# Scattering the expert gates: products of four tokens side by side in PSUM, part of the marks on ScalarE, small marks for 48 tokens

## The chip, the cores and the metric

The kernel runs on one core of one Trainium2 chip. The metric is the device time of one execution in microseconds. TensorE does the matmuls and writes PSUM; VectorE (DVE), ScalarE (ACT) and GpSimd (POOL) work on 128 partitions at a time; SyncE (SP) issues most DMAs. Each engine runs its own instructions in order, and the engines wait for one another through semaphores.

## The reference

Two transformer blocks over 512 tokens of width 1024. The changed code lies in the feed-forward layer of the first, a product-key mixture of 16384 experts:

```
s = einsum('thpc,hpnc->thpn', q, keys)            # two scores of 128 keys for each of 8 heads
v1, i1 = top_k(s[:, :, 0], 16);  v2, i2 = top_k(s[:, :, 1], 16)
sc, pos = top_k(v1[..., :, None] + v2[..., None, :], 16)     # over 256 pairs
idx = (i1 * 128 + i2) at pos;  gate = softmax(sc)
act = gelu(einsum('td,thkd->thk', x, u_tab[idx]))
out = einsum('thk,thkd->td', gate * act, v_tab[idx])
```

So each token chooses 8 x 16 = 128 experts, each with two coordinates (i1, i2) of 0 to 127 and a gate.

## The kernel before

For three of the four blocks of 128 tokens (ND = 384) the kernel does not gather expert rows. It runs all experts densely: for each of 128 values of the second coordinate, `up` makes the 128 x 384 products with `pe_u` and their Gelu, `dense` multiplies them with the gates and with `pe_v`. For that it needs the gates as a full matrix of 128 x 128 experts for each token, zero where an expert is not chosen. `scatter` builds it.

At its start `slots` holds, with the 128 chosen experts on the partitions and the 384 tokens along the row: 0 the gate, 1 and 2 the upper three bits (0 to 7) and the lower four bits (0 to 15) of the first coordinate, 3 the second coordinate. `iota` is a row of 0 to 127. For a token, `e[0]` is the matrix (chosen expert x first coordinate) with the gate at the mark, `e[1]` the matrix (chosen expert x second coordinate) with a one at the mark. One TensorE matmul of the two sums over the chosen experts and gives the 128 x 128 gates of this token.

The loop goes over 24 blocks of 16 tokens (`t16`) and in each over 4 quads of four tokens (`q`), 96 quads in all:

- per block, on VectorE: `g` (L518, L522), the upper bits' marks times the gates, 16 x 8 numbers, and `lw` (L520), the lower bits' marks, 16 x 16 in bf16;
- per quad, on VectorE: `e[1]` (L527), a comparison of 4 x 128 elements, and `e[0]` (L529), the product of `g` and `lw` spread over 4 x 8 x 16 elements. The two tiles have three buffers each;
- per quad, on TensorE: four f32 matmuls of 128 x 128 into one PSUM bank `p` (L534). In the trace each is two records. Four banks (role `gp`) take turns;
- per quad, on ScalarE: three copies of 10 values of the second coordinate each to `gm` (L537), which stays in SBUF for the first RES = 30 values, and one copy of the other 98 to `out` (`go`, L538). In SBUF the token is the innermost index, in `p` the second coordinate is, so these copies write single f32 apart from each other;
- per block, SP's queue stores `out` to DRAM (L540). `dense` loads it later in groups (L549 to L552).

The generator yields after each quad, and `interleave` puts the remaining steps of `fill` between the quads. `fill` is `ahead`: the `up` work of the first EARLY = 26 values of the second coordinate, 24 f32r matmuls each, with the load and split of its weights (L62, L64, L67) and a Gelu (L566). The program is then ordered for each engine by a scheduler with its own estimate of the durations, so quads and `up` work need not follow each other as the loop has them. When the last quad is copied, `dense` begins: L608 multiplies the early Gelus with rows of `gm`, each a row of all 384 tokens.

Of the kernel before, what the change touches and what calls it, by code (L numbers as in the profile page):

```python
# [13 lines left out]
F32 = mybir.dt.float32  # L14
# [3 lines left out]
BF16 = mybir.dt.bfloat16  # L18
AF = mybir.ActivationFunctionType
ALU = mybir.AluOpType  # L20
# [327 lines left out]
ND = 384  # L348
NB = ND // 16
RES, GRP = 30, 8  # L350
# [70 lines left out]
class Peer:  # L421
# [84 lines left out]
    def scatter(self, wk, ps, slots, pool, iota):  # L506

        k, nc = self.k, self.k.nc
        V, A, G, T = nc.vector, nc.scalar, nc.gpsimd, nc.tensor
        for t16 in range(NB):
            ts = slice(16 * t16, 16 * t16 + 16)
            g = pool.tile([128, 16, 8], F32, name=k.name("gu"), tag="gu")
            lw = pool.tile([128, 16, 16], BF16, name=k.name("lw"), tag="lw")
            out = pool.tile([128, 128 - RES, 16], F32, name=k.name("go"), tag="go")
            V.tensor_tensor(out=g, in0=slots[:, 1, ts].unsqueeze(2).to_broadcast([128, 16, 8]),  # L518
                            in1=iota[:, 0:8].unsqueeze(1).to_broadcast([128, 16, 8]), op=ALU.is_equal)
            V.tensor_tensor(out=lw, in0=slots[:, 2, ts].unsqueeze(2).to_broadcast([128, 16, 16]),  # L520
                            in1=iota[:, 0:16].unsqueeze(1).to_broadcast([128, 16, 16]), op=ALU.is_equal)
            V.tensor_tensor(out=g, in0=g, in1=slots[:, 0, ts].unsqueeze(2).to_broadcast([128, 16, 8]), op=ALU.mult)  # L522
            for q in range(4):
                o = 16 * t16 + 4 * q
                e = [wk.tile([128, 512], F32, name=k.name("e"), tag=tag, bufs=3).rearrange("p (t n) -> p t n", t=4)
                     for tag in ("alo", "ahi")]
                V.tensor_tensor(out=e[1], in0=slots[:, 3, o:o + 4].unsqueeze(2).to_broadcast([128, 4, 128]),  # L527
                                in1=iota.unsqueeze(1).to_broadcast([128, 4, 128]), op=ALU.is_equal)
                V.tensor_tensor(out=e[0].rearrange("p t (u l) -> p t u l", u=8),  # L529
                                in0=g[:, 4 * q:4 * q + 4].unsqueeze(3).to_broadcast([128, 4, 8, 16]),  # L530
                                in1=lw[:, 4 * q:4 * q + 4].unsqueeze(2).to_broadcast([128, 4, 8, 16]), op=ALU.mult)
                p = ps.tile([128, 4, 128], F32, name=k.name("gp"), tag="gp")
                for i in range(4):
                    T.matmul(p[:, i, :], e[0][:, i, :], e[1][:, i, :], start=True, stop=True)  # L534
                n = RES // 3
                for z in range(3):
                    A.copy(self.gm[z][:, :, o:o + 4].rearrange("p n t -> p t n"), p[:, :, n * z:n * z + n])  # L537
                A.copy(out[:, :, 4 * q:4 * q + 4].rearrange("p n t -> p t n"), p[:, :, RES:])  # L538
                yield
            nc.sync.dma_start(self.gd[t16], out.rearrange("p n t -> p (n t)"))  # L540

# [1652 lines left out]
```

## Time and profile before

| | us |
|---|---|
| median of 3 runs | 3055.88 (3053.62 to 3061.26) |
| the profiled execution's own time | 3059.69 |
| its span, first to last instruction | 3057.9 |
| PE busy | 2931.2 (96%) |
| DVE busy | 2066.5 (68%) |
| ACT busy | 1374.2 (45%) |
| POOL busy | 645.4 (21%) |

An engine's busy time is the sum over all stages. Since the stages have different limits, a stage is read from the windows, which give each engine's busy time in a stretch, and from the chain of waits, which goes back from the last instruction to what released it. In the lists a group has the line of the kernel, the engine, the operation, the tile written and those read, the shapes and the count. Starts of successive instructions on one engine can lie closer together than the recorded duration, since an instruction begins before the last results of the one ahead are written.

### The profile page before, as it was taken

The page shows a single profiled execution, that of the slowest core. Times are in us where ns is not written, and L with a number is a line of the kernel's source. Part 1 is how long each engine was busy: PE and PEld are TensorE (multiplying, and loading weights), DVE is VectorE, ACT ScalarE, POOL GpSimd, SP SyncE. Part 2 cuts the span into 40 slices and gives each one's busy share as a digit, 9 for nine tenths or more (in the row PEclk, how much of TensorE's full clock was granted, in tenths as well). Part 3 has the DMA queues.
Part 4 walks back from the last instruction along what each step waited for, and adds up shares of the span by engine and source line. Part 5 has one row for each costly group of instructions (what it writes and reads, how often), then busy time and mean ns, then how long its engine had stood idle before and what let it go on. Part 6 is the DMA issues. An engine that isn't in the chain of part 4 may idle for free.

```text
span 3057.9 us, 45818 instructions
## 1 busy us (share of the span) xinstructions
PE 2931.2 (96%) x17602; PEld 2489.1 (81%) x17602; DVE 2066.5 (68%) x4031; ACT 1374.2 (45%) x2543; POOL 645.4 (21%) x435
## 2 busy tenths in 40 slices
PE   8888989998899999999999999989999999999999
PEld 6766779997688999999999987668888877888887
DVE  6877768989997888888886446675552653655522
ACT  5444453357533333333333355664442554554422
POOL 0000014400004444444442011002222121012220
PEclk9898999999999999999999999999999999999999
DMA  2000252243349999999996432323223442133222
GB/s 96 26 21 30 80 182 92 90 149 151 151 147 329 342 334 334 340 337 330 331 334 243 130 116 70 110 91 105 97 97 104 161 133 92 53 105 97 97 96 83
DMA packets 177787, 481.86 MB, mean 158 GB/s; under 512 B 18944, under 2 KB 68864, under 8 KB 177312
## 3 DMA queue, kind: packets, MB, share of 16 engines
q1 hardware_dynamic: 140704, 344.70, 33.3%
q0 software_dynamic: 36864, 134.23, 12.1%
q8 instruction: 138, 2.26, 0.3%
q14 instruction: 81, 0.66, 0.1%
HBM read 454.36 MB, written 24.51 MB: 157 GB/s over the span
## 4 chain that ended last, share of the span: by engine, by line
PE 74%; DVE 7%; ACT 1%; issue 1%; DMA 1%; POOL 0%; DVEq 0%; ACTq 0%
PE pacc L119 6%; PE pu L117 6%; PE pu L119 6%; PE pu L118 6%; PE pacc L118 5%; PE pacc L117 5%; PE up L118 5%; PE up L119 5%; PE up L117 5%; PE acc L117 3%; PE acc L118 3%; PE acc L119 3%; PE pj L117 2%; PE pj L118 2%; PE pj L119 2%; PE sp L805 2%
## 5 line engine op out<-in xcount | busy, mean ns | idle before, releaser
L64 ACT CAST whi<-raw 128x1024 fp32r<-128x1024 f32 x505 | 529.6, 1050 | 686.8 <-PE pu L118 184.0
L67 DVE TENSOR_TENSOR wlo<-raw,whi 128x1024 fp32r<-128x1024 f32 x394 | 487.9, 1240 | 473.6 <-ACT whi L64 468.0
L67 POOL TENSOR_TENSOR wlo<-raw,whi 128x1024 fp32r<-128x1024 f32 x111 | 273.2, 2463 | 1057.1 <-ACT whi L64 1028.5
L117 PE MATMUL pu<-pe_hhi,whi 128*128 128x384 f32 x1024 | 348.4, 340 | 1.5 <-ACT gl L566 1.5
L119 PE MATMUL pu<-pe_hhi,wlo 128*128 128x384 f32 x1024 | 346.8, 339 | 0.5 <-DVE wlo L67 0.5
L118 PE MATMUL pu<-pe_hlo,whi 128*128 128x384 f32 x1024 | 346.9, 339 | 0.0
L118 PE MATMUL pacc<-wlo,ahi 128*128 128x512 f32 x768 | 304.2, 396 | 0.7 <-DVE wlo L67 0.7
L117 PE MATMUL pacc<-whi,ahi 128*128 128x512 f32 x768 | 295.6, 396 | 1.7 <-ACT ahi L610 1.5
L119 PE MATMUL pacc<-whi,alo 128*128 128x512 f32 x768 | 290.2, 398 | 3.3 <-DVE alo L611 3.3
L118 PE MATMUL up<-res_h,whi 128*128 128x512 f32 (+1 forms) x752 | 282.7, 376 | 0.1
L117 PE MATMUL up<-res_h,whi 128*128 128x512 f32 (+1 forms) x752 | 282.5, 377 | 0.0
L119 PE MATMUL up<-res_h,wlo 128*128 128x512 f32 (+1 forms) x752 | 282.1, 376 | 0.0
L639 POOL DMA_INDIRECT row<-pe_rows,pe_gs x128 | 163.2, 1275 | 212.2 <-DVE pe_gs L646 177.3
L639 POOL DMA_INDIRECT row<-pe_v,pe_gs x128 | 166.2, 1299 | 187.7 <-DVE pe_acc L655 175.0
L259 DVE SCALAR_TENSOR_TENSOR u<-up,ffn_par,u 128x511 f32<-128x511 f32 (+1 forms) x176 | 131.5, 748 | 104.7 <-ACT u L257 101.7
L117 PEld LDWEIGHTS pu<-pe_hhi,whi 128*128 128x128 f32 x1024 | 192.7, 188 | 6.5 <-ACT gl L566 1.8
L118 PEld LDWEIGHTS pu<-pe_hlo,whi 128*128 128x128 f32 x1024 | 192.8, 188 | 4.3
L119 PEld LDWEIGHTS pu<-pe_hhi,wlo 128*128 128x128 f32 x1024 | 192.7, 188 | 1.2 <-DVE wlo L67 0.8
L119 PEld LDWEIGHTS pacc<-whi,alo 128*128 128x128 f32 x768 | 145.0, 189 | 38.2 <-DVE alo L611 3.8
L118 PEld LDWEIGHTS pacc<-wlo,ahi 128*128 128x128 f32 x768 | 144.8, 189 | 32.1 <-DVE wlo L67 1.2
L117 PEld LDWEIGHTS pacc<-whi,ahi 128*128 128x128 f32 x768 | 144.6, 189 | 31.6 <-ACT ahi L610 1.7
L655 DVE SCALAR_TENSOR_TENSOR pe_acc<-row,pe_gs,pe_acc 128x1024 f32<-128x1024 f32 x128 | 164.0, 1281 | 6.6 <-DMA row<-pe_v,pe_gs 6.4
(505 smaller groups left out, 6207.6 us busy)
## 6 DMA issues: line engine op xcount, KB each, us to landing
raw<-pe_u SPq DMA_DIRECT2D x128, 512.0 KB
raw<-pe_v SPq DMA_DIRECT2D x128, 512.0 KB
raw<-ffn_up SPq DMA_DIRECT2D x88, 512.0 KB
raw<-ffn_dn SPq DMA_DIRECT2D x55, 512.0 KB
pe_gd<-go SPq DMA_DIRECT2D x24, 784.0 KB
gc<-pe_gd SPq DMA_DIRECT2D x12, 1536.0 KB
mraw<-mx_in SPq DMA_DIRECT2D x80, 128.0 KB
raw<-pe_wq SPq DMA_DIRECT2D x16, 512.0 KB
```

What stands on the lines that cost most here:

```text
L64: nc.scalar.copy(hi, raw)
L67: eng.tensor_tensor(out=lo, in0=raw, in1=hi, op=ALU.subtract)
L117: mm(out, l[0], r[0], start=first, stop=False)
L118: mm(out, l[0], r[1], start=False, stop=False)
L119: return mm(out, l[1], r[0], start=False, stop=last)
L259: V.scalar_tensor_tensor(out=u[:, d:], in0=p[:, :S - d], scalar=par[:, o + 2 - d:o + 3 - d], in1=u[:, d:], op0=ALU.mult, op1=ALU.add)
L639: G.indirect_dma_start(out=r, out_offset=None, in_=table[z], in_offset=bass.IndirectOffsetOnAxis(ap=idx[:, j:j + 1], axis=0))
L655: V.scalar_tensor_tensor(out=acc, in0=row("v", j), scalar=w[:, j:j + 1], in1=acc, op0=ALU.mult, op1=ALU.add)
L805: nc.tensor.matmul(p[:, :w], lhs, rhs, start=True, stop=True)
```

## The change

Three things in `scatter`:

- The four matmuls of a quad write `p[:, :, i]` of a bank laid out as (second coordinate, token) instead of (token, second coordinate), so a matmul's 128 columns are four f32 apart, and the four products lie side by side. The copies read the bank in order and write four adjacent f32 for each value of the second coordinate.
- In every third quad (32 of 96) `e[1]` is made by ScalarE: for each of the four tokens |iota - coordinate| with a per-partition bias from `minus`, then for all 512 elements relu(1 - that).
- `g` and `lw` are made once for three blocks (48 tokens). `lw` has the token innermost, (16, 48), and is made from bf16 copies of the bits (`low`) and of the numbers 0 to 15 (`rep`); `e[0]` reads it across, with the 16 values innermost and 48 elements from one to the next. `minus`, `low` and `rep` are made once ahead of the loop.

```diff
+        minus = pool.tile([128, ND], F32, name="pe_minus", tag="minus", bufs=1)
+        V.tensor_scalar(out=minus, in0=slots[:, 3], scalar1=-1.0, scalar2=None, op0=ALU.mult)
+        low = pool.tile([128, ND], BF16, name="pe_low", tag="low", bufs=1)
+        V.tensor_copy(low, slots[:, 2])
+        rep = pool.tile([128, 16, 48], BF16, name="pe_rep", tag="rep", bufs=1)
+        V.tensor_copy(rep, iota[:, 0:16].unsqueeze(2).to_broadcast([128, 16, 48]))
         for t16 in range(NB):
-            ts = slice(16 * t16, 16 * t16 + 16)
-            g = pool.tile([128, 16, 8], F32, name=k.name("gu"), tag="gu")
-            lw = pool.tile([128, 16, 16], BF16, name=k.name("lw"), tag="lw")
+            if t16 % 3 == 0:
+                ts = slice(16 * t16, 16 * t16 + 48)
+                g = pool.tile([128, 48, 8], F32, name=k.name("gu"), tag="gu")
+                lw = pool.tile([128, 16, 48], BF16, name=k.name("lw"), tag="lw")
+                V.tensor_tensor(out=g, in0=slots[:, 1, ts].unsqueeze(2).to_broadcast([128, 48, 8]),
+                                in1=iota[:, 0:8].unsqueeze(1).to_broadcast([128, 48, 8]), op=ALU.is_equal)
+                V.tensor_tensor(out=lw, in0=low[:, ts].unsqueeze(1).to_broadcast([128, 16, 48]), in1=rep,
+                                op=ALU.is_equal)
+                V.tensor_tensor(out=g, in0=g, in1=slots[:, 0, ts].unsqueeze(2).to_broadcast([128, 48, 8]), op=ALU.mult)
             out = pool.tile([128, 128 - RES, 16], F32, name=k.name("go"), tag="go")
...
             for q in range(4):
-                o = 16 * t16 + 4 * q
+                o, i3 = 16 * t16 + 4 * q, 16 * (t16 % 3) + 4 * q
...
-                V.tensor_tensor(out=e[1], in0=slots[:, 3, o:o + 4].unsqueeze(2).to_broadcast([128, 4, 128]),
-                                in1=iota.unsqueeze(1).to_broadcast([128, 4, 128]), op=ALU.is_equal)
+                if (4 * t16 + q) % 3 == 2:
+                    for i in range(4):
+                        A.activation(e[1][:, i, :], iota, AF.Abs, bias=minus[:, o + i:o + i + 1])
+                    A.activation(e[1], e[1], AF.Relu, scale=-1.0, bias=1.0)
+                else:
+                    V.tensor_tensor(out=e[1], in0=slots[:, 3, o:o + 4].unsqueeze(2).to_broadcast([128, 4, 128]),
+                                    in1=iota.unsqueeze(1).to_broadcast([128, 4, 128]), op=ALU.is_equal)
                 V.tensor_tensor(out=e[0].rearrange("p t (u l) -> p t u l", u=8),
-                                in0=g[:, 4 * q:4 * q + 4].unsqueeze(3).to_broadcast([128, 4, 8, 16]),
-                                in1=lw[:, 4 * q:4 * q + 4].unsqueeze(2).to_broadcast([128, 4, 8, 16]), op=ALU.mult)
-                p = ps.tile([128, 4, 128], F32, name=k.name("gp"), tag="gp")
+                                in0=g[:, i3:i3 + 4].unsqueeze(3).to_broadcast([128, 4, 8, 16]),
+                                in1=lw[:, :, i3:i3 + 4].rearrange("p l t -> p t l").unsqueeze(2)
+                                .to_broadcast([128, 4, 8, 16]), op=ALU.mult)
+                p = ps.tile([128, 128, 4], F32, name=k.name("gp"), tag="gp")
                 for i in range(4):
-                    T.matmul(p[:, i, :], e[0][:, i, :], e[1][:, i, :], start=True, stop=True)
+                    T.matmul(p[:, :, i], e[0][:, i, :], e[1][:, i, :], start=True, stop=True)
                 n = RES // 3
                 for z in range(3):
-                    A.copy(self.gm[z][:, :, o:o + 4].rearrange("p n t -> p t n"), p[:, :, n * z:n * z + n])
-                A.copy(out[:, :, 4 * q:4 * q + 4].rearrange("p n t -> p t n"), p[:, :, RES:])
+                    A.copy(self.gm[z][:, :, o:o + 4], p[:, n * z:n * z + n, :])
+                A.copy(out[:, :, 4 * q:4 * q + 4], p[:, RES:, :])
                 yield
```

## Rows read from the trace of the kernel before

**Rows 1.** Windows: stretch, length; busy us of PE, PEld, DVE, ACT, POOL; clock; DMA.
```profile
649.60:697.00 47.40, 47.40 (x328) 47.40 (x327) 38.65 (x69) 28.89 (x87) 0.00 (x0) 1.00 0.43 155
697.00:803.00 106.00, 82.34 (x618) 73.12 (x616) 104.22 (x203) 82.98 (x314) 0.00 (x0) 1.00 0.37 150
```

**Rows 2.** Chain of waits, 680 to 812 us: start, us, engine, tile, line.
```profile
689.53 2.68 PE gp L534 x24
...
715.77 0.34 DVE lw L520
...
718.51 0.20 DVE gu L522
...
721.66 0.60 DVE e L527
722.26 0.60 DVE e L529
...
726.88 0.34 DVE lw L520
...
802.88 1.57 DVE gl L608 x4
```

**Rows 3.** Window of line L534 alone, PE and PEld.
```profile
649.60:697.00 47.40, 18.40 (x152) 18.41 (x153) 1.00 0.43 155
```

**Rows 4.** Groups of VectorE by line and shape: count, busy us, mean ns.
```profile
L527 DVE TENSOR_TENSOR e<-pe_slots,pe_iota 128x512 f32<-128x512 f32 x96 | 64.7, 683 | 3.0 <-PE gp L534 3.0
L608 DVE TENSOR_TENSOR gl<-gl,gc 128x384 f32<-128x384 f32 x98 | 54.3, 554 | 33.3 <-ACT gl L566 29.7 <-issue 2.6
L520 DVE TENSOR_TENSOR lw<-pe_slots,pe_iota 128x256 bf16<-128x256 f32 x24 | 10.0, 416 | 0.0
```

**Rows 5.** Timeline of ScalarE, 712 to 718 us: start, us, line, operation.
```profile
712.15 0.45 ACT L537 COPY gm<-gp 128x40 f32<-128x40 f32 x3
712.41 0.89 ACT L538 COPY go<-gp 128x392 f32<-128x392 f32 x1
713.06 0.46 ACT L537 COPY gm<-gp 128x40 f32<-128x40 f32 x3
```

**Rows 6.** Lines L413 and L416 (VectorE, bf16): duration ns minimum/median/maximum.
```profile
L413 DVE TENSOR_TENSOR big<-ijf,iota x32: 660/680/1694, 483.2 to 918.5; 128x512 bf16<-128x512 bf16 x32
L416 DVE TENSOR_TENSOR big<-big,f x32: 364/422/2617, 484.6 to 919.2; 128x512 bf16<-128x512 bf16 x32
```

**Rows 7.** VectorE where it reads across: groups by shape, and line L1840.
```profile
L1834 DVE TENSOR_TENSOR P<-P 128x225 f32<-128x225 f32 x4 | 2.2, 546 | 0.1
L1836 DVE TENSOR_REDUCE P<-P 128x15 f32<-128x225 f32 x4 | 1.5, 386 | 0.1
L1834 DVE TENSOR_TENSOR P<-P 128x81 f32<-128x81 f32 x4 | 1.2, 292 | 0.1
...
L1840 DVE TENSOR_SCALAR TT<-P,mx_cst x16: 343/391/442, 104.6 to 344.2; 128x256 f32<-128x256 f32 x16
```

**Rows 8.** ScalarE: timelines at three other places, and a group.
```profile
1850.27 0.40 ACT L813 ACTIVATE s<-s,st 128x128 f32<-128x128 f32 x1 [5.64 <-DVE st L806]
1850.58 0.19 ACT L813 ACTIVATION_READ_ACCUMULATOR s<-s,st 128x1 f32 x1
...
1860.67 0.95 ACT L827 COPY pT<-tp 128x384 f32<-128x384 f32 x2
...
2506.64 0.31 ACT L1157 ACTIVATE sz<-sz 128x128 f32<-128x128 f32 x1
2506.99 0.31 ACT L1158 ACTIVATE sz<-sz 128x128 f32<-128x128 f32 x1
...
2557.20 0.63 ACT L1158 ACTIVATE sz<-sz 128x512 f32<-128x512 f32 x1
...
L827 ACT COPY pT<-tp 128x512 f32<-128x512 f32 x32 | 18.4, 585 | 14.7 <-PE tp L825 14.4
```

**Rows 9.** Chain of waits, 814 to 830 us.
```profile
818.89 0.23 PE pacc L117
```

More of the change, by code (lines that the diff above doesn't have):

```diff
@@ L511, in scatter @@
         k, nc = self.k, self.k.nc
-        V, A, G, T = nc.vector, nc.scalar, nc.gpsimd, nc.tensor
-        for t16 in range(NB):
-            ts = slice(16 * t16, 16 * t16 + 16)
-            g = pool.tile([128, 16, 8], F32, name=k.name("gu"), tag="gu")
-            lw = pool.tile([128, 16, 16], BF16, name=k.name("lw"), tag="lw")
-            out = pool.tile([128, 128 - RES, 16], F32, name=k.name("go"), tag="go")
[L518 to L522, printed above, removed]
+        V, A, T = nc.vector, nc.scalar, nc.tensor
```

## The prediction

> **What bounds the kernel now.** The views in this order. The windows by stage come first: the changed function, `scatter`, runs from 649 to 803 us, and there are two stretches in it. From 649.6 to 697 TensorE is busy without a gap and VectorE is not (38.65 of 47.40 us). From 697 to 803 it is the other way round: VectorE 104.22 of 106.00 us, TensorE 82.34, ScalarE 82.98 [rows 1]. The chain of waits says the same: TensorE's runs of `gp` up to 697, then an unbroken series of VectorE's `e` (L527, L529), `gu` and `lw` until the last quad's matmuls and copies and the first L608, which reads `gm`, at 802.88 [rows 2]. L608 needs a row of all 384 tokens, so the stage's end is a barrier: what `scatter` gains or loses, the kernel does.
>
> The window of L534 gives the counts [rows 3]: of 768 matmul records for 96 quads of four tokens, 8 a quad, 152 (19 quads) lie before 697; with the one under way I count 20 quads before and 76 behind. In the second stretch the pattern in the chain repeats every two blocks of 16 tokens: `lw` at 715.77 and again at 726.88, so 11.11 us for 8 quads, 1.389 us a quad [rows 2]. That is VectorE's work alone: two 512-element instructions that start 0.60 us apart, 1.20, and once per block of 16 tokens `gu`, `lw`, `gu` with 0.20 + 0.34 + 0.20 = 0.74 us, 0.185 a quad [rows 2]. Intervals count here: each instruction starts 0.08 us before the recorded duration of the one ahead (683 and 416 ns [rows 4]) is over. TensorE alone needs 0.89 us a quad (2.68 for 24 records [rows 2]). ScalarE, where it has a backlog, needs 0.26 for the three `gm` copies and 0.65 for `go`, 0.91 [rows 5].
>
> **The change, part by part.** *A third of the second marks to ScalarE.* VectorE loses 32 of 96 L527, 0.60/3 = -0.20 us a quad.
>
> *Small marks for 48 tokens.* Now a set costs 0.74 us per 16 tokens, 2.23 per 48. The two `gu` instructions get 384 elements: an L608 of that size lasts 554 ns [rows 4], so 0.47 as interval. `lw` gets 768 bf16 elements, all three operands bf16 with step one. L416, of that kind with 512, has a minimum of 364 and a median of 422 ns where L413, one of whose operands repeats an element, has 660 and 680 [rows 6]: half the time per element. So 768 cost 0.47 us (0.87 if the double rate fails). Set: 1.40 us, gain 0.83 per 12 quads, -0.07 a quad (-0.04 at worst). The three new instructions ahead of the loop (`minus`, `low`, `rep`) are 384, 384 and 768 elements, about 1.5 us by the same rows; TensorE is then in `up` work without a gap, so they cost nothing, and 1.5 us if that cover were gone.
>
> *The first marks, L529.* Same count, same 512 elements, but `lw` now lies with the token innermost and is read across it: step 48 bf16 elements, 96 bytes, for each element. No row shows that step. The nearest is L1834, a VectorE TENSOR_TENSOR whose first input steps by 16 f32 (64 bytes): 225 elements last 546 ns and 81 last 292, 1.76 ns an element, where the contiguous L1836 of 225 lasts 386 [rows 7]. The other row is L1840, half of whose instances read with that step in an op of one tensor: 442 against 343 ns for 256, +0.39 ns an element [rows 7]. L529 now runs at 0.683 - 0.150 = 0.533 us for 512, 1.04 ns. Bounds: nothing (if the 16 addresses that it repeats eight times cost no more than now) and twice L1834's extra; a gain is excluded, since it has as many elements and no faster mode with an f32 input. I take L1834, the same op: (1.76 - 1.04) x 512 = +0.37 us a quad.
>
> The Trainium skill ("Vector Engine (DVE) Microarchitecture Reference", § 5.2 Measured stream behaviour on trn2) has the full rate only for runs of two adjacent words, 1.73 ns an element where one source hops, and 2.50 where both sources or the output step by 24 words. Our step is 24 words; the trace bears out 1.76 at 16 words and has nothing at 24. By 2.50 the term would be +0.75.
>
> *Sum for VectorE:* 1.389 - 0.200 - 0.069 + 0.370 = 1.490 us a quad, +0.10.
>
> *ScalarE.* The copies now read `p` in order and write runs of four f32 instead of single ones 64 bytes apart. `go` had 0.65 us for 392 elements; a contiguous L827 copy of 384 from PSUM starts its successor 0.36 us later (two span 0.95, the second, of 512, has 0.59) [rows 8]. So 0.26 + 0.36 = 0.62 a quad; if the runs don't help, 0.91. The marks: an activation of 128 with a pointer operand holds the engine 0.31 us (L813 at 1850.27, next at 1850.58), a dependent one follows 0.35 behind a 311 ns one, and 512 take 0.63, 0.55 as interval [rows 8]. Three at 0.31, the fourth 0.43 because the Relu reads it, and 0.55: 1.9 us for a marked quad. Per three quads 3 x 0.62 + 1.9 = 3.76, 1.25 a quad (1.54 if the copies stay as they are). This hides under VectorE's 1.49. If Abs and Relu needed other tables than Gelu, loads would come only where Gelus lie between, before 697, where ScalarE has 18.5 us idle [rows 1].
>
> *TensorE.* Each matmul writes its 128 columns 16 bytes apart. No row shows a strided PSUM output. The f32r matmuls of the next stage write a column every 0.45 ns (512 in 0.23 us [rows 9]), these f32 passes one every 0.87 (128 in 0.112), so a port that takes single words at half the best rate would still keep up: I take 0. The other end is twice the time, 0.89 us more a quad.
>
> *Moved or queued:* the 24 stores on SP's queue and POOL's queue are as before. The marked quads put 1.9 us of ScalarE ahead of copies that release PSUM; with four banks and 1.49 us a quad that is 6 us of room.
>
> **Total.** Before 697 TensorE sets the pace and VectorE has 8.75 us idle against +2 us; nothing changes. Behind it 76 quads x 0.10 = +7.6 us. If the altered order makes VectorE the limit over all 96 and shows the head too, +9.6 + 1.5 = +11.1. I take +9. The profiled execution took 3059.69 us (its span 3057.9 and 1.8 around it), 3.8 over the median of the runs; the step applies to either: 3055.9 + 9 = 3065 us.
>
> **Rivals.**
> *R1, reads cost nothing or L1840's price.* For it: the addresses of a token repeat eight times; against: L1834. VectorE would need 1.12 a quad and ScalarE's 1.25 be the limit: 76 x -0.14 = -10.6, 3045; with L1840's price VectorE needs 1.32, 76 x -0.07 = -5, 3051; if ScalarE packs its 132 us (96 x 0.62 + 61 + 11 for `up`) from 655 on, 3040. It decides from where L529's interval is under 0.87 us.
> *R2, the wide step costs twice L1834's extra*, +0.74: VectorE 1.86 a quad, 76 x 0.47 = +36, over all 96 quads +45: 3092 to 3101. For it: the step is wider than any in the trace; against: L1834 already jumps at every element. The 2.50 ns above would be this case.
> *R3, strided PSUM writes slow TensorE.* At the ratio of L1834 (1.69) a quad takes 1.51, at twice 1.79. Before 697 that is 20 quads x 0.62 to 0.89 = 12 to 18 us at once, since TensorE is the limit there; behind it 76 x (1.51 to 1.79 less 1.389) = 9 to 30: 3077 to 3104, centre 3088. It decides from 1.49 us a quad. Against it stands the half-rate argument from rows 9. The Trainium skill ("PSUM — Partial Sum Buffer", § Specifications (TRN2)) says that any non-contiguous access pattern slows matmuls significantly; no run so far shows it.
> *R4, the copies don't get faster*: ScalarE at 1.54 a quad, just over VectorE: 76 x 0.15 = +11.5, 3067; it changes the forecast by little and is counted with it.
>
> **Chances.** Forecast with R4 0.36 (3060 to 3070), R1 0.28, R2 0.20, R3 0.16. About 0.3% (9 us) can be told from no change. The forecast lies on that edge: half within, half slower. R1: 0.20 faster, 0.08 within. R2 and R3 slower. So faster 0.20, same 0.26, slower 0.54. Range: down to 3044, where most of R1 is in, up to 3096, which leaves out the upper thirds of R2 and R3; about 0.2 lies outside.
>
> **What would show it.** L529's interval in a run of them: 0.97 (forecast), 0.6 to 0.8 (R1), 1.34 (R2). The gap between `gp` groups where TensorE has a backlog: 0.89, or 1.5 and more (R3). `go`'s duration: 0.49 or still 0.87. `lw` of 768: about 0.5 us. The four Abs and one Relu: 1.9 us. The window that ends at the first L608: 8 to 11 us later. I am wrong if L529 keeps 683 ns, or if the stage ends on ScalarE's copies rather than on VectorE's marks.

## The result and the profile after

The changed kernel takes 3110.13 us (median of 4 runs, 3105.90 to 3111.08) where the kernel before takes 3058.57 beside it (3053.62 to 3063.76): a ratio of 1.0162 with a 95% interval of 1.0147 to 1.0177, so 1.6% slower. The forecast was 3065 with a range up to 3096; the time lies 14 us above the range and 9 above the top of rival R2 (3092 to 3101).

| us | before | after |
|---|---|---|
| the profiled execution's span | 3057.9 | 3107.8 |
| first L608 (after: L622), the barrier behind `scatter` | 802.88 | 846.43 |
| last `up` matmul (L119) of the second feed-forward | 2927.1 | 2977.4 |
| matmuls of L1068 (after: L1082), first to last | 1964.0 to 2028.9 | 2005.5 to 2078.3 |

So +43.5 us at the barrier and +50.3 at the end. The last row says where the other 7 or 8 are: one stretch of the attention far behind, which the change doesn't touch, takes 72.8 us instead of 64.9. The two are looked at one after the other. Behind the changed function every line number is 14 higher than before.

The windows of the kernel after, in the columns of [rows 1], up to the barrier, which is now at 846 us:

```profile
652.00:690.00 38.00, 37.94 (x259) 37.52 (x257) 37.69 (x38) 26.62 (x92) 0.00 (x0) 1.00 0.41 146
690.00:846.40 156.40, 103.88 (x669) 95.33 (x667) 148.66 (x149) 106.44 (x464) 0.00 (x0) 0.87 0.28 110
```

VectorE has 37.69 of 38.00 us and 148.66 of 156.40: it is all but full from the first quads on. Up to 690 TensorE is full beside it (37.94), as it was before 697 in [rows 1], where VectorE had room. Of the 7.7 us that VectorE lacks behind 690, 4.6 are its wait for the last quads' matmuls and copies at the barrier. The groups of VectorE, columns as in [rows 4], say which instruction:

```profile
L541 DVE TENSOR_TENSOR e<-gu,lw 128x512 f32<-128x512 f32 x96 | 135.0, 1430 | 0.3 <-PE gp L548 0.3
L539 DVE TENSOR_TENSOR e<-pe_slots,pe_iota 128x512 f32<-128x512 f32 x64 | 43.8, 687 | 2.9 <-PE gp L548 2.7
L524 DVE TENSOR_TENSOR gu<-pe_slots,pe_iota 128x384 f32<-128x384 f32 x8 | 4.4, 555 | 0.2
L526 DVE TENSOR_TENSOR lw<-pe_low,pe_rep 128x768 bf16<-128x768 bf16 x8 | 4.3, 551 | 0.0
```

L541 is the old L529: the same 512 elements, 1430 ns instead of 683 [rows 4]. The second marks keep 687 ns, 64 of them are left, and `lw` has its double rate (551 ns for 768 where 256 took 416 before [rows 4]). VectorE's timeline (start, us, engine, line, operation) gives the intervals:

```profile
727.67 0.56 DVE L524 TENSOR_TENSOR gu<-pe_slots,pe_iota 128x384 f32<-128x384 f32 x1
728.15 0.55 DVE L526 TENSOR_TENSOR lw<-pe_low,pe_rep 128x768 bf16<-128x768 bf16 x1
728.62 0.69 DVE L539 TENSOR_TENSOR e<-pe_slots,pe_iota 128x512 f32<-128x512 f32 x1
729.22 1.43 DVE L541 TENSOR_TENSOR e<-gu,lw 128x512 f32<-128x512 f32 x1
730.56 0.55 DVE L528 TENSOR_TENSOR gu<-gu,pe_slots 128x384 f32<-128x384 f32 x1
```

L541 starts at 729.22 and its successor at 730.56: 1.34 us, where two neighbours of [rows 2] are 0.60 apart. L539 takes 0.60, `gu` 0.48, `lw` 0.47. The whole stage on VectorE is 96 x 1.34 + 64 x 0.60 + 8 x (0.48 + 0.47 + 0.47) = 178.4 us, 1.86 a quad, which is the sum of R2.

ScalarE's copies did become faster, as its timeline shows beside [rows 5]:

```profile
732.59 1.30 ACT L536 ACTIVATE e<-pe_iota,pe_minus 128x128 f32<-128x128 f32 x4
733.77 0.39 ACT L551 COPY gm<-gp 128x40 f32<-128x40 f32 x3
734.01 0.54 ACT L552 COPY go<-gp 128x392 f32<-128x392 f32 x1
734.39 0.45 ACT L551 COPY gm<-gp 128x40 f32<-128x40 f32 x3
734.64 0.58 ACT L552 COPY go<-gp 128x392 f32<-128x392 f32 x1
735.02 0.73 ACT L537 ACTIVATE e<-e 128x512 f32<-128x512 f32 x1
```

`go` starts at 734.01 and its successor at 734.39: 0.38 us instead of 0.65. The four Abs take 1.18 and a Relu some 0.54 with a backlog behind it: 1.72 for the marks of a quad.

The chain of waits has the barrier and, where TensorE has a backlog at full clock, its price per quad:

```profile
658.60 2.68 PE gp L548 x24
...
713.49 4.45 PE gp L548 x24
...
846.43 1.56 DVE gl L622 x4
```

2.68 us for 24 records is the number of [rows 2] to the digit, although each column now lands 16 bytes from the last. The 4.45 at 713 is the same work at a lowered clock, as two neighbouring windows show (columns of [rows 1]):

```profile
712.00:718.00 6.00, 4.43 (x24) 4.17 (x24) 5.66 (x6) 2.99 (x14) 0.00 (x0) 0.72 0.34 137
718.00:724.00 6.00, 3.01 (x24) 2.83 (x24) 6.00 (x6) 5.22 (x23) 0.00 (x0) 1.00 0.33 135
```

24 records at full clock (2.4 GHz) take 3.01 us and at a mean of 0.72, part of the time at 1.2 GHz, 4.43. TensorE stood waiting for VectorE ahead of the slow run. Since VectorE has 5.66 and 6.00 us of 6.00 in the two windows, and its marks wait 3.0 us for TensorE in the whole stage, this costs the stage little.

### The profile page after: what moved, and what is told of

The parts are those of the page before. It is cut to its first block, busy times and chain, and to the rows that moved or that the text cites. A ratio compares the mean times of both kernels' runs of the same rounds, so it can differ in the third digit from the quotient of the medians.

```text
span 3107.8 us, 45890 instructions
## 1 busy us (share of the span) xinstructions
PE 2954.5 (95%) x17602; PEld 2508.8 (81%) x17602; DVE 2113.2 (68%) x3954; ACT 1399.2 (45%) x2703; POOL 650.8 (21%) x435
## 4 chain that ended last, share of the span: by engine, by line
PE 74%; DVE 7%; issue 1%; ACT 1%; DMA 1%; POOL 0%; DVEq 0%; ACTq 0%; SPq 0%
PE pacc L119 5%; PE pacc L118 5%; PE pacc L117 5%; PE pu L117 5%; PE pu L118 5%; PE pu L119 5%; PE up L117 5%; PE up L119 5%; PE up L118 5%; PE acc L118 3%; PE acc L117 3%; PE acc L119 3%; PE pj L117 2%; PE pj L118 2%; PE pj L119 2%; DVE e L541 2%
## 5 line engine op out<-in xcount | busy, mean ns | idle before, releaser
L119 PE MATMUL pu<-pe_hhi,wlo 128*128 128x384 f32 x1024 | 347.4, 339 | 0.2 <-DVE wlo L67 0.2
L119 PE MATMUL pacc<-whi,alo 128*128 128x512 f32 x768 | 290.2, 398 | 3.4 <-DVE alo L625 3.4
L119 PE MATMUL up<-res_h,wlo 128*128 128x512 f32 (+1 forms) x752 | 282.6, 376 | 0.0
L119 PEld LDWEIGHTS pu<-pe_hhi,wlo 128*128 128x128 f32 x1024 | 192.7, 188 | 0.8 <-DVE wlo L67 0.5
L119 PEld LDWEIGHTS pacc<-whi,alo 128*128 128x128 f32 x768 | 145.0, 189 | 38.2 <-DVE alo L625 3.9
```

The lines of the kernel that those rows point to most:

```text
L119: return mm(out, l[1], r[0], start=False, stop=last)
```

## Experiments

The theory: the loss is the read across of `lw` in the first marks (96 bytes from element to element). Rivals: the writes into PSUM; ScalarE's marks; something in how the three meet. Each run stands beside runs of the kernel before on the same chip (medians 3057.9 to 3060.2). "Group" in the expectations is a quad of four tokens.

**1. The read across undone** in the changed kernel: `lw` lies token by token and is read two bytes apart. It is made from `slots` and `iota` again, as before the change, at 950 ns for 768 elements instead of 551; `low` and `rep` are gone.

```diff
-                lw = pool.tile([128, 16, 48], BF16, name=k.name("lw"), tag="lw")
+                lw = pool.tile([128, 48, 16], BF16, name=k.name("lw"), tag="lw")
...
-                                in1=lw[:, :, i3:i3 + 4].rearrange("p l t -> p t l").unsqueeze(2)
+                                in1=lw[:, i3:i3 + 4].unsqueeze(2)
```

> The changed kernel with one thing undone: lw lies token by token again (48 x 16), so that the first marks read it in order; PSUM layout, ScalarE's marks and the sets for 48 tokens stay. Theory (the read across at 96 bytes is the whole loss): the first marks fall from 1430 to 683 ns, VectorE needs 0.60 + 0.40 + 0.15 = 1.15 us a quad, ScalarE 0.64 + 1.8/3 = 1.24, so the stage runs at 1.24 instead of 1.389 and the kernel takes 3042 to 3050 us, 8 to 15 under the kernel before. Rival (the waits between ScalarE's marks, TensorE at its lower clock and VectorE make the loss): the stage keeps most of its 44 us, 3085 us and more.

Measured: 3065.59 us, ratio 1.0020 (1.0011 to 1.0030). The first marks are back at 685 ns and 45 of the 50 us are gone, so the read across is the loss. The gain that should then have been left (3042 to 3050 was expected) is not there: the barrier is at 804.37. The chain of this run shows what holds it:

```profile
739.67 1.17 PE gp L544 x8
740.87 0.38 ACT gm L547 x3
741.25 0.39 ACT go L548
741.64 1.16 ACT e L532 x4
742.80 0.55 ACT gm L547 x6
743.36 0.40 ACT go L548
743.80 1.17 PE gp L544 x8
744.99 0.38 ACT gm L547 x3
745.38 0.39 ACT go L548
745.77 1.16 ACT e L532 x4
747.20 0.40 ACT go L548
747.64 1.17 PE gp L544 x8
```

A loop of TensorE and ScalarE without VectorE: matmuls of a quad, its copies, the Abs of a later quad, copies, and the next matmuls, 4.13 and 3.84 us for two turns (739.67 to 743.80 to 747.64) of three quads each: 1.33 a quad (every fourth turn goes by VectorE's small marks and takes 4.70), where ScalarE's own work is (3 x 0.64 + 1.70) / 3 = 1.21 and VectorE's less. `ahi`, the tag of the second marks, has three buffers, and ScalarE marks every third quad: its quads always get the same one. So I formed a second theory, a ring: Abs of quad k + 3 waits for the matmuls of quad k. The trace shows the loop, but not that buffer. What waits in it is TensorE, for `go` copies (all that the two share is a bank of `p`), and ScalarE's `gm` copies for TensorE; no Abs shows a wait for TensorE. If the buffer holds the loop, it does so by the place that it leaves for the Abs in ScalarE's order. The first of the waits here and in experiment 5 (who waits, for whom: us in all, times, longest):

```profile
PE gp L544 <- ACT go L548: 17.4, 16, 1.6
...
PE gp L546 <- ACT go L550: 3.2, 9, 0.7
```

**2. The read across alone**, put into the kernel before (VectorE makes all second marks, PSUM and copies as before).

> The kernel before with the sets for 48 tokens read across alone; all second marks on VectorE, products one behind the other in PSUM as before. Theory: first marks 1430 ns, VectorE 0.60 + 1.35 + 0.12 = 2.07 us a quad, 0.68 more than before: 96 x 0.68 = 65 us less about 8 of VectorE's idle time before 697 us, 3112 to 3124 us. Rival (waits and clock): without ScalarE's marks in the loop little is lost, 3065 us or less.

Measured: 3116.37 us, ratio 1.0177 (1.0157 to 1.0197), in the expected range. The windows, and the group:

```profile
655.00:697.00 42.00, 39.75 (x268) 38.05 (x267) 42.00 (x47) 24.94 (x77) 0.00 (x0) 1.00 0.37 126
697.00:802.00 105.00, 72.97 (x424) 64.30 (x424) 105.00 (x114) 57.65 (x204) 0.00 (x0) 0.84 0.28 113
```
```profile
L539 DVE TENSOR_TENSOR e<-gu,lw 128x512 f32<-128x512 f32 x96 | 135.8, 1417 | 0.0
```

VectorE is busy in all of 147.00 us. This one edit makes the whole loss and more: its barrier is at 861.52, 15 us behind that of the whole change; in the medians it is 6 us, which the intervals don't separate (the traced execution, 3123.16 us, is the slowest of four).

**3. The layout in PSUM alone**, put into the kernel before: `p` as (128, 4), the matmuls to `p[:, :, i]`, the copies in order.

> The kernel before with the products side by side in PSUM and the copies in order alone. Theory: matmul records keep their 0.112 us in a run, the copy to go falls from 870 to 530 ns, and since VectorE sets the pace nothing is gained: 3053 to 3061 us. Rival (strided PSUM writes slow TensorE): 0.19 us or more a record, 3080 us.

Measured: 3061.03 us, ratio 1.0005 (0.9995 to 1.0014). The group of the matmuls in this run:

```profile
L534 PE MATMUL gp<-e,e 128*128 128x128 f32 x768 | 100.7, 280 | 23.2 <-DVE e L529 20.2 <-ACT go L538 0.9
```

100.7 us for 768 in the kernel before too, 280 ns each: the writes 16 bytes apart cost TensorE nothing. The Trainium skill ("PSUM — Partial Sum Buffer", § Specifications (TRN2)) has it that any non-contiguous pattern slows matmuls significantly; for these f32 matmuls the measurement decides, and it shows nothing. `go` falls from 884 to 519 ns, and that is worth nothing as long as VectorE is the limit.

**4. The read by itself:** the kernel before with 26 extra products on VectorE ahead of the scatter, each of 512 elements like the first marks, whose second operand is read with one step each. The one with 96 bytes:

```diff
+        V.tensor_tensor(out=res, in0=one, in1=wide[:, 0:768].rearrange("p (l w) -> p l w", w=48)[:, :, 0:4].rearrange("p l t -> p t l").unsqueeze(2).to_broadcast([128, 4, 8, 16]), op=ALU.mult)
```

> The kernel before with 26 more VectorE products ahead of scatter, of the same form as the first marks (512 elements, one operand repeated), whose other operand steps by 1 to 128 bf16 or 1 to 64 f32. Theory A (24 words is a bad step among others): 1430 ns at 48 bf16 and at 24 f32, about 1050 (1.76 ns an element) at 32 bf16 and 16 f32 and at the wide ones. Rival B (the cost grows with the step): 1050 at 16 words, 1430 at 24, more from 32 on. Rival C (the first marks are slow for the mixture of types): f32 steps cost less than bf16 steps of the same bytes. Steps under 8 bytes should cost nothing in all.

Measured (one run; its whole time is of no use here): durations in ns of each product (minimum, median, maximum of one). First bf16 with steps of 2, 8, 16, 64, 96 and 128 bytes, then f32 with steps of 4, 64 and 96 bytes:

```profile
L517 DVE TENSOR_TENSOR mb_res<-pe_iota,mb_wide x1: 679/679/679, 642.1 to 642.1; 128x512 f32<-128x512 f32 x1
L518 DVE TENSOR_TENSOR mb_res<-pe_iota,mb_wide x1: 678/678/678, 643.3 to 643.3; 128x512 f32<-128x512 f32 x1
L519 DVE TENSOR_TENSOR mb_res<-pe_iota,mb_wide x1: 1060/1060/1060, 645.3 to 645.3; 128x512 f32<-128x512 f32 x1
L522 DVE TENSOR_TENSOR mb_res<-pe_iota,mb_wide x1: 1043/1043/1043, 648.7 to 648.7; 128x512 f32<-128x512 f32 x1
L524 DVE TENSOR_TENSOR mb_res<-pe_iota,mb_wide x1: 1419/1419/1419, 656.0 to 656.0; 128x512 f32<-128x512 f32 x1
L527 DVE TENSOR_TENSOR mb_res<-pe_iota,mb_wide x1: 1095/1095/1095, 665.2 to 665.2; 128x512 f32<-128x512 f32 x1
L531 DVE TENSOR_TENSOR mb_res<-pe_iota,mb_wide x1: 672/672/672, 678.4 to 678.4; 128x512 f32<-128x512 f32 x1
L535 DVE TENSOR_TENSOR mb_res<-pe_iota,mb_wide x1: 1030/1030/1030, 689.2 to 689.2; 128x512 f32<-128x512 f32 x1
L537 DVE TENSOR_TENSOR mb_res<-pe_iota,mb_wide x1: 1421/1421/1421, 696.3 to 696.3; 128x512 f32<-128x512 f32 x1
```

Less the 150 ns that the prediction takes off, an element costs 1.03 ns with steps up to 8 bytes, 1.74 at 64 bytes, 1.85 at 128, and 2.48 at 96, the same for bf16 and f32. The other steps measured (16 to 256 bytes) lie at 1.7 to 2.1, and 100 bytes at 2.21: 96 is the worst of all that were tried. At 64 bytes it is L1834's 1.76 [rows 7] again: the row was read rightly and carried to a step where it doesn't hold. The Trainium skill ("Vector Engine (DVE) Microarchitecture Reference", § 5.2) gives 2.50 for steps of 24 words, there for both sources or the output; here one source alone has it.

**5. The ring broken by buffers:** experiment 1 with two buffers of their own for ScalarE's marks.

```diff
+                mine = (4 * t16 + q) % 3 == 2
...
-                     for tag in ("alo", "ahi")]
-                if (4 * t16 + q) % 3 == 2:
+                     for tag in (("alo",) if mine else ("alo", "ahi"))]
+                if mine:
+                    e.append(pool.tile([128, 4, 128], F32, name=k.name("am"), tag="am", bufs=2))
```

> The small marks token by token, read 2 bytes apart (as in the first experiment), and the marks that ScalarE makes written into two buffers of their own instead of the three that all groups share. Theory (the ring of shared buffers held the first experiment: every third group's buffer is the same one, so ScalarE's marks for group k+3 wait for the matmuls of group k): the ring is gone, ScalarE's own work of 3.62 us per three groups (three times 0.64 of copies, 1.16 of Abs, 0.54 of Relu) sets the pace, 1.21 us a group, the first product of the last group's wait comes some 10 to 14 us earlier than in the first experiment (barrier near 790 to 795 us), time 3047 to 3056. Rival (the ring is not in these buffers but in ScalarE's order itself, copies of group k behind marks of a later one): nothing moves, barrier 803 to 806, time 3062 to 3067.

Measured: 3048.99 us, ratio 0.9968 (0.9958 to 0.9978); barrier at 787.92, 16.5 us earlier than in experiment 1. The windows of the two, first experiment 1, then this:

```profile
697.00:803.00 106.00, 75.36 (x609) 70.12 (x609) 88.67 (x142) 96.82 (x436) 0.00 (x0) 1.00 0.37 151
```
```profile
697.00:780.00 83.00, 72.16 (x561) 66.38 (x560) 78.66 (x128) 82.86 (x383) 0.00 (x0) 1.00 0.42 169
```

In the first no engine is full; in the second ScalarE has 82.86 of 83.00 us, and TensorE's waits for `go` are down from 17.4 to 3.2 us. So the shared buffers did hold experiment 1. Why is less sure: the second marks have five buffers here instead of three, and this run doesn't tell whether three were too few or whether it mattered that ScalarE always got the same one.

**6. Another step in the changed kernel:** 128 bytes instead of 96, by longer rows.

```diff
-                lw = pool.tile([128, 16, 48], BF16, name=k.name("lw"), tag="lw")
+                lw = pool.tile([128, 16, 64], BF16, name=k.name("lw"), tag="lw")[:, :, 0:48]
```

> The changed kernel with one size altered: a row of the small marks' tile is 64 columns long instead of 48, so that the first marks read theirs 128 bytes apart instead of 96; instructions, counts and order of the code are the same. Theory (the loss lies in the 96-byte step alone, 2.48 ns an element where steps of 64 and 128 bytes cost about 1.75): the first marks fall from 1.35 us to 1.05 to 1.10, VectorE's work in the stage from 189 us to 160 to 165, barrier near 815 to 825, time 3075 to 3090 (some 25 us less than the changed kernel; the forecast's own price in place). Rival (any read across costs as much inside this stage): first marks stay at 1.35 us, time 3105 to 3115.

Measured: 3079.38 us, ratio 1.0067 (1.0050 to 1.0084), 31 us less than the changed kernel by 16 columns that nothing reads. Its first marks:

```profile
L541 DVE TENSOR_TENSOR e<-gu,lw 128x512 f32<-128x512 f32 x96 | 99.6, 1064 | 1.8 <-PE gp L548 1.6
```

1064 ns, an interval of some 0.98 us, which is the forecast's 0.97 in place. But the barrier is at 821.50, +18.6 us and not the +9 of the forecast: the forecast would have been too low even with its price right. The trace has part of the rest: the first mark starts at 653.00 instead of 649.57, and VectorE's marks wait 7.1 us for TensorE instead of 3.0. Whether the ring makes these waits wasn't tried in this kernel.

**7. A step of 8 bytes:** `lw` as (12 quads, 16, 4), still made by one instruction at double rate (`rep` and that instruction follow the layout).

```diff
-                lw = pool.tile([128, 16, 48], BF16, name=k.name("lw"), tag="lw")
+                lw = pool.tile([128, 12, 16, 4], BF16, name=k.name("lw"), tag="lw")
...
-                                in1=lw[:, :, i3:i3 + 4].rearrange("p l t -> p t l").unsqueeze(2)
+                                in1=lw[:, i3 // 4].rearrange("p l t -> p t l").unsqueeze(2)
```

> The changed kernel with the small marks laid out group by group (12 groups, 16 low parts, 4 tokens): the single instruction for 48 tokens keeps its double rate, and the first marks read 8 bytes apart instead of 96. Theory (steps up to 8 bytes are free, and what holds is then ScalarE's ring): first marks 0.68 us, small marks about 0.55 us for 48 tokens, barrier 800 to 806, time 3058 to 3067, as the first experiment. Rival (VectorE was what bound the first experiment): the 0.4 us a group-of-twelve that double rate saves shows, 4 us under the first experiment.

Measured: 3070.39 us (3063.62 to 3071.86), ratio 1.0038 (1.0023 to 1.0052), 3 us over the expected range; the barrier at 802.33 is where it was expected. The traced execution took 3063.62, the shortest of five, and lies in the range: where the runs of 3070 to 3072 lose their time is not shown. First marks 686 ns, `lw` 551.

**8. The ring broken by the count:** experiment 7 with every fourth quad on ScalarE (`% 4 == 2`), in the shared buffers.

> As the experiment with the 8-byte step, but ScalarE makes the marks of every fourth group instead of every third, still in the three shared buffers, so that its groups take the three buffers in turn. Theory (the ring comes from three buffers and every third group falling together): the ring is gone; VectorE then needs 0.60 + 0.75 x 0.60 + 0.12 = 1.17 us a group and ScalarE (4 x 0.64 + 1.70) / 4 = 1.07, so the stage runs at about 1.17 to 1.2 a group instead of 1.39: barrier near 787 to 793 us, time 3043 to 3053. Rival (the ring is in ScalarE's order or the matmuls at lowered clock): barrier 800 to 806, time 3058 to 3067.

Measured: 3054.46 us (3048.58 to 3059.02), ratio 0.9986 (0.9975 to 0.9997), barrier 792.48, 10 us earlier than in experiment 7, with less work taken from VectorE. It fits the ring, and here the number of buffers stayed at three; but ScalarE's smaller load shortens a loop too. Experiment 5 kept the load and changed the number, this one kept the number and changed the load: no run changes only which buffer ScalarE's quads get. The time is 1.5 us over the expected range; the attention behind the barrier takes 5.2 us more than before (last table).

**9. The marks alone**, put into the kernel before.

> The kernel before with one part of the change alone: a third of the second coordinate's marks made by ScalarE; products in PSUM, copies and small marks are the old ones. Theory (ScalarE has no room for the marks while its copies take 0.92 us a group): its work becomes 0.92 + 1.70 / 3 = 1.49 us a group against 1.39 of the whole stage before, with the shared buffers' ring on top; barrier 812 to 820 instead of 803, time 3066 to 3078. Rival (VectorE alone sets the pace and gains 0.20 us a group): barrier near 785 to 790, time 3043 to 3050.

Measured: 3080.57 us, ratio 1.0075 (1.0060 to 1.0091), barrier 821.93: the direction of the theory, some 2 us worse than its range. From 697 to 780 us ScalarE is busy 76.43 of 83.00 us there, VectorE 64.25. So the marks need the room that the faster copies of the PSUM layout give, although these are worth nothing alone; how much of the loss is the ring's was not separated.

**10. The three cures together:** experiment 7's layout, own buffers, and 2 of 7 quads on ScalarE.

```diff
+                mine = (4 * t16 + q) % 7 in (2, 5)
...
+                        A.activation(e[1][:, i, :], iota, AF.Abs, scale=-1.0,
+                                     bias=slots[:, 3, o + i:o + i + 1])
```

> The three cures together: small marks read 8 bytes apart, ScalarE's marks in two buffers of their own, and 2 of 7 groups marked by ScalarE (its Abs takes the minus sign from its scale, which saves the tile of negated indices). Theory: VectorE 0.60 + 5/7 x 0.60 + 0.12 = 1.15 us a group, ScalarE 0.65 + 2/7 x 1.70 = 1.14, so the stage runs at 1.15 to 1.18 a group, under the 1.21 of the run with ScalarE at a third; barrier 780 to 786, time 3040 to 3048 with some 5 to 7 us lost again in the attention behind, as in every kernel whose order there is another. Rival (two engines at one pace wait for each other, or TensorE is in the way): no better than the run with own buffers at a third, 787 and 3049.

Measured: 3038.13 us (3036.23 to 3044.49), ratio 0.9936 (0.9922 to 0.9949): 0.6% faster than before and 2.3% faster than the change. Barrier at 781.63. The window:

```profile
697.00:780.00 83.00, 76.15 (x595) 70.42 (x595) 80.39 (x136) 81.08 (x379) 0.00 (x0) 1.00 0.46 179
```

Three engines at 76 to 81 of 83 us: nothing much is left to shift. The loss in the attention, which I had expected to come back, did not (below).

**11. The order behind:** the kernel before with one memset of 512 columns on VectorE ahead of the scatter.

```diff
+        wide = pool.tile([128, 512], F32, name="wide", tag="wide", bufs=1)
+        for _ in range(1):
+            V.memset(wide, 1.0)
```

> The kernel before with one memset of a 128 x 512 tile on VectorE ahead of the scatter, about 0.3 us of work: nothing else of the code is altered, but the order of the instructions in the attention far behind comes out different, as in every kernel of this study whose time lines differ. Theory (the 5 to 8 us lost there come from the order alone, not from the scatter): the stretch between the end of the peer stage and the feed-forward takes 1 to 8 us longer than before, at unchanged scatter; time 3058 to 3067. Rival (the loss there is bound to the scatter's change): no difference behind the scatter beyond 0.5 us, time within 1 us of before.

Measured: 3059.30 us, ratio 1.0004 (0.9995 to 1.0013). The run didn't do what it was meant to. In the traces, told apart by line, operation, tiles and shape, every instruction of TensorE, VectorE and ScalarE behind the barrier stands in the order of before. And the scatter is not unchanged: the barrier is at 800.32 instead of 802.88 (in experiment 3, with VectorE's work as before, at 805.00; so 2 or 3 us at the barrier are not to be read as an effect). The matmuls of the old L1068 take 66.7 us instead of 64.9 in the same order. The time can't be told from before.

For the 7 us behind the barrier the lines of these matmuls were read in every run (counts, minimum, median and maximum in ns, first and last start). Before, after, experiment 7 and experiment 10:

```profile
L1068 PE MATMUL po<-pT,ev_dv x80: 271/275/579, 1964.0 to 2028.9; 128*128 128x128 f32 x80
```
```profile
L1082 PE MATMUL po<-pT,ev_dv x80: 270/275/582, 2005.5 to 2078.3; 128*128 128x128 f32 x80
```
```profile
L1083 PE MATMUL po<-pT,ev_dv x80: 270/275/582, 1959.3 to 2032.2; 128*128 128x128 f32 x80
```
```profile
L1084 PE MATMUL po<-pT,ev_dv x80: 271/275/582, 1942.3 to 2007.8; 128*128 128x128 f32 x80
```

| kernel | order of the attention | its stretch, us | granted clock in it |
|---|---|---|---|
| before, 3, 11 | that of before | 64.9, 65.5, 66.7 | 1.00, 1.00, 0.97 |
| 10, 2 | that of before on TensorE and ScalarE, another on VectorE | 65.5, 68.7 | 1.00, 0.94 |
| 4 | its own | 67.0 | 1.00 |
| 1, 5, 8, 9 | a second | 69.8, 71.5, 70.1, 70.3 | 0.91, 0.89, 0.91, 0.91 |
| after, 6, 7 | a third | 72.8, 72.7, 72.9 | 0.89, 0.89, 0.89 |

The stretch is the last start less the first; the clock is that of a window of 60 us around it; the orders are those of the stretch and the 130 us ahead of it, instances of one line not told apart. The changed kernel and experiments 6 and 7 have barriers at 846, 821 and 802 us, the same order of the attention, and the same 72.8 us: so the 7 or 8 us don't go with what `scatter` gains or loses. They go with the order in part: three orders have three bands. But experiments 10 and 2 have one order and take 65.5 and 68.7 us. In every row but that of experiment 4 the lower clock has the longer stretch. An edit ahead of the attention can bring it a new order, as in the changed kernel, and need not, as in experiments 3 and 11. The rows of before and after:

```profile
1970.00:2030.00 60.00, 52.69 (x252) 34.09 (x252) 48.70 (x142) 44.73 (x120) 0.00 (x0) 1.00 0.21 72
```
```profile
2013.00:2073.00 60.00, 55.17 (x214) 33.50 (x214) 45.19 (x134) 41.31 (x109) 0.00 (x0) 0.89 0.22 70
```

Fewer matmuls (214 against 252) in as long a window, at a clock of 0.89. Whether the order lowers the clock, or is slow for a cause of its own, stays open: no run was made in which the order alone is another.

## Why the prediction was wrong

**The step that failed** is the price of the first marks' read across: "I take L1834, the same op: (1.76 - 1.04) x 512 = +0.37 us a quad." It is +0.74 (interval 1.34 for 0.60, the sign that the prediction gives for R2; 2.48 ns an element by itself in experiment 4). The text had both ends, "nothing" and "twice L1834's extra", and took the row "nearest" to it, with a chance of 0.20 for the other. Nearest in bytes is not nearest in cost: 64 and 128 bytes cost 1.74 and 1.85, 96 between them 2.48. The row for it could not be had from the trace; the one figure that named the step, 24 words, was left to R2.

**R2 was right** in price (1.86 a quad, summed here again at 178.4 us for 96) and at the barrier: it said +36 to +45, measured +43.5. Its price was twice the extra of another row, and no reason was given for the two but the 2.50 ns; that it fits to 0.01 us is in part luck. The forecast's "nothing changes" before 697 fell with it: at 1.86 VectorE is full there too. Most of what R2's 3101 lacks of 3110 is the attention's 7 to 8 us, which no part of the text had.

**A step that was missing** is the ring. The text priced engines and said of the marked quads that "with four banks and 1.49 us a quad that is 6 us of room": it looked at PSUM's four buffers and not at the three of `ahi`, of which ScalarE's quads use one. In the changed kernel this costs little, since VectorE is full; it shows where the reads are free, and there the room is gone too (TensorE waits 17.4 us for `go` in experiment 1). With the reads free, R1 gave 3040 to 3051 for ScalarE's 1.25 a quad; experiments 1 and 7 have free reads and show 3066 and 3070, since ScalarE and TensorE wait for each other at some 1.33 a quad. With the ring gone R1's numbers come true (3049, ScalarE full). So R1's condition was too short: it needed cheap reads and buffers.

**Right:** `lw` of 768 at 0.47 us, as said; `gu` 0.48 for 0.47; `go` 0.38 for 0.36, so R4 falls; the marks 1.72 for 1.9; no cost on TensorE from the writes, so R3 falls (experiment 3). The half-rate argument for it was not tested beyond this case.

**The range** ended at 3096, which leaves out more than half of R2's 3092 to 3101 and not the upper third that the prediction says. With R2's price bounded by a row whose step is 32 bytes away, its top of 3101 should have been in; the attention's 7 to 8 us would have needed a margin that only the experiments showed.

## What to carry to other kernels

Layout for the engine that is the limit: an operand that its costliest instruction reads is laid out for that read (steps up to 8 bytes were free here), and if the writer wants tokens innermost, make the runs short (groups of four) rather than the step long. A step between two measured ones is not bounded by them; when one cost doubles by it, give that case the weight of the forecast. Where two engines take turns in a set of buffers, count which buffer each turn gets: taken in turn, every third task on three buffers is one buffer, and every fourth is three. Two buffers more took 16.5 us off the stage here.

## What was not expected of the hardware

- VectorE's product with one operand read 96 bytes apart costs 2.48 ns an element (1419 ns for 512), at 64 and 128 bytes 1.74 and 1.85; widening the row by 16 unread columns took 31 us off the kernel.
- Steps of 8 bytes in bf16 cost nothing (678 against 679 ns), steps of 16 bytes already 1060 ns.
- TensorE's f32 matmuls wrote PSUM in columns 16 bytes apart at 280 ns a record, the same as adjacent ones; ScalarE's copy of 392 f32 in runs of four took 519 ns and in single words 64 bytes apart 884.
- The same attention code took 64.9 to 72.9 us, at granted clocks of 1.00 to 0.89, in kernels that differ only far ahead of it; in one and the same order it took 65.5 us at 1.00 and 68.7 at 0.94.
